# The first column of a block in the token mix, made by ScalarE instead of VectorE

## The chip, the core and the metric

The kernel runs on one core of one Trainium2 chip. The time is device microseconds from one launch to its end. The core's engines each work through their own queue of instructions in order: TensorE (PE in the profile, with its weight loads as PEld), VectorE (DVE), ScalarE (ACT), GpSimd (POOL), and SyncE (SP), which issues all the transfers here. An instruction that needs another engine's result waits at the head of its queue, and what stands behind it waits too.

## What is computed

One hybrid decoder layer on a sequence of 2048 tokens of width 1024, after an embedding layer norm: an input projection, RWKV-7 time mixing on eight heads, forgetting attention on eight heads, a SiLU gate, an output projection and a final layer norm. What matters here is the token mix of the projection's RWKV part: each token is mixed with the one before.

```python
h = x * (1.0 + scale[:, None, :]) + shift[:, None, :]
proj = h @ w_in
rw = proj[..., :RW_END]
rw_prev = jnp.pad(rw, ((0, 0), (1, 0), (0, 0)))[:, :-1]
rw = rw + (rw_prev - rw) * rwkv_mix        # r, k, v, and the two low-rank inputs
...                                        # decay, keys, scan over tokens, group norm
S = S * w_t - (S kk_t) b_t^T + v_t k_t^T   # the recurrence per head
```

## The kernel before

The sequence is worked in two halves of 1024 tokens, each half in two blocks of 512. The projection runs as tiles of 128 features by 512 tokens: 24 matmuls of 128x512 add up into one PSUM bank (three for each of eight slices of the inner dimension, since the operands are split into a rounded part and a rest). The tiles are written with features on partitions and tokens along the free axis, so "the token before" is the column to the left.

When the 24 matmuls of a tile are done, an evacuation stream takes the bank. For the parts r, k, v and the low-rank inputs this is `shift_mix` (line 901): ACT writes the bank times (1 - mix) into an SBUF slot of the tile `arena`; DVE adds the bank's columns 0 to 510 times mix to columns 1 to 511; DVE adds the last column of the block before, kept in the tile `car`, times mix to column 0; DVE copies the bank's column 511 into `car` for the next block; the bank is freed. `par("mix", g)` is a column of the tile `params`, one factor per partition. There are 13 feature groups, 2 halves and 2 blocks, so 52 calls. A weight tile is loaded by `weights` (line 818): a DMA into `wst`, an ACT cast into `wsp`, and a POOL subtraction (128x1024) that makes the rest; the projection matmuls read `ht` and `wsp`.

The recurrence (tiles `rw_s`, `rw_l`, `state`) runs beside the projection: per head group and block elementwise work, a triangular solve (`rwkv_solve`, line 1271: a long chain of small DVE instructions that ends in two transposes, then matmuls of 32x16 and of 32x32), and state updates by 64x64 matmuls (`rwkv_batch`, line 1361). Each pair of heads and half has two such solves, here called the first and the second of a pair. Attention works on `fx_s`, `fx_p` and `fx_v`.

No order is written by hand: a planner inside the kernel (`Driver`, from line 138) runs all streams as coroutines against a model of the engines. It gives each instruction a cost (`cost`, line 167) by engine, size, whether an operand lies in PSUM, and how many operands are pointers, adds a latency from one engine to another, and always goes on with the stream that is ready first. The order in which streams emit instructions is the order in which each engine's queue holds them. So a change of one instruction's engine changes the model's times, and with them the order of all that follows.

The program's calls go through one helper, so all instructions bear the line 134 and are told apart by tile names. `ps` is PSUM.

Of the kernel before, what the change touches and what calls it, by code (L numbers as in the profile page):

```python
# [12 lines left out]
AF = mybir.ActivationFunctionType  # L13
OP = mybir.AluOpType
# [274 lines left out]
def hymba_kernel(ctx: ExitStack, tc, x, c, emb_ln_g, emb_ln_b, w_ada, b_ada, w_in, rwkv_mix, w0,  # L289
# [3 lines left out]
    pe, act, dve, pool, sp = (Engine(drv, n, e) for n, e in (("pe", nc.tensor), ("act", nc.scalar),  # L293
                              ("dve", nc.vector), ("pool", nc.gpsimd), ("sp", nc.sync)))
# [73 lines left out]
    car = const.tile([128, 16], F32, name="car")  # L368
# [37 lines left out]
    def par(name, i=0):  # L406
        return params[:, off[name] + i:off[name] + i + 1]
# [493 lines left out]
    def shift_mix(b, g, o):  # L901

        act.activation(o, b.ap, AF.Copy, scale=pc[:, g:g + 1])
        yield
        dve.scalar_tensor_tensor(o[:, 1:512], b.ap[:, 0:511], par("mix", g), o[:, 1:512],
                                 op0=OP.mult, op1=OP.add)
        dve.scalar_tensor_tensor(o[:, 0:1], car[:, g:g + 1], par("mix", g), o[:, 0:1],
                                 op0=OP.mult, op1=OP.add)
        dve.tensor_copy(car[:, g:g + 1], b.ap[:, 511:512])
        b.free()  # L910
        yield

    def ev_low(b, half, p, blk):
        lo = yield from slots.get(1)
        yield from shift_mix(b, 12, lo.ap)
        act.activation(lo.ap[0:64], lo.ap[0:64], AF.Tanh)
        yield
        low[half, blk] = lo
# [60 lines left out]
    def ev_r(k, g0):  # L979
        def ev(b, half, p, blk):  # L980
            s = yield from slots.get(1)
            if blk:
                pending[0] -= 1
            if k == "g":
                yield from silu(b, s)
            else:
                yield from shift_mix(b, g0 + p, s.ap)
            res[half, p, k, blk] = s
        return ev
# [1069 lines left out]
```

## Time and profile before

| | us |
|---|---|
| three runs | 1901.69, 1914.04, 1914.87; median 1914.04 |
| the profiled execution | 1905.47 |
| its span, first to last instruction | 1903.7 |
| PE matmuls busy / PE weight loads | 1816.7 / 1307.2 |
| DVE busy | 1287.7 |
| ACT busy | 802.5 |
| POOL busy | 778.2 |
| mean granted clock of TensorE | 0.968 |

Busy times of different engines overlap, so they don't add up. The granted clock is a share of full speed: 1 is 2.4 GHz, 0.5 is 1.2 GHz, and a value between is a mean over both. The profiled execution is one run of its own, beside the three.

### The profile page before, as it was taken

What the parts mean: (1) busy time and instruction counts of PE and PEld (TensorE: products, weight loads), DVE (VectorE), ACT (ScalarE), POOL (GpSimd) and SP (SyncE); (2) the same over time, 40 slices, a digit from 0 to 9 for tenths busy, and PEclk for the clock granted to TensorE, in tenths of its full rate; (3) what the DMA queues carried; (4) which work ended last, traced back from release to release, by engine and by line L of the source; (5) the groups of instructions that cost most, each with busy time, mean ns of one, the idle gap of its engine ahead of it and who ended that gap; (6) DMA issues with size and microseconds to landing.
All of it is one profiled execution on the core that took longest, in us unless ns stands there. A gap on an engine that the chain in (4) does not pass through costs nothing. (4 is left out here: it accounts for less than half of the span.)

```text
span 1903.7 us, 35535 instructions
## 1 busy us (share of the span) xinstructions
PE 1816.7 (95%) x13609; PEld 1307.2 (69%) x13609; DVE 1287.7 (68%) x3049; ACT 802.5 (42%) x1573; POOL 778.2 (41%) x773
## 2 busy tenths in 40 slices
PE   8988999989999999999998999999999999999997
PEld 6766777767678657577776777777655557457775
DVE  6887376856645555857667764754678722897998
ACT  3454445554541543554554653452444431441000
POOL 2222341514222573624142333423456651485553
PEclk9999999999889999999999999999999999799999
DMA  9241110201116537232020111214433217413333
GB/s 293 66 123 52 42 53 21 64 24 45 61 42 188 171 115 234 84 118 72 13 72 24 46 39 40 72 56 129 125 116 107 87 62 251 157 62 121 133 134 105
DMA packets 172129, 181.60 MB, mean 95 GB/s; under 512 B 12180, under 2 KB 116197, under 8 KB 171960
## 3 DMA queue, kind: packets, MB, share of 16 engines
q1 hardware_dynamic: 171960, 179.33, 30.3%
q8 instruction: 108, 1.77, 0.4%
q14 instruction: 61, 0.50, 0.1%
HBM read 132.10 MB, written 47.13 MB: 94 GB/s over the span
## 5 line engine op out<-in xcount | busy, mean ns | idle before, releaser
L134 PE MATMUL ps<-ht,wsp 128*128 128x512 f32 x3840 | 985.9, 403 | 9.4 <-POOL wsp L134 7.5
L134 PEld LDWEIGHTS ps<-ht,wsp 128*128 128x128 f32 x3840 | 703.8, 190 | 167.6 <-issue 12.1
L134 POOL TENSOR_TENSOR wsp<-wst,wsp 128x1024 fp32r<-128x1024 f32 x79 | 195.4, 2473 | 331.0 <-ACT wsp L134 303.3
L134 ACT ACTIVATE rw_s<-ps 64x256 f32<-64x256 f32 (+3 forms) x544 | 215.6, 408 | 212.6 <-PE ps L134 111.9
L134 PE MATMUL ps<-rw_s 32*32 32x32 f32 (+4 forms) x5376 | 238.7, 227 | 34.1 <-DVE rw_s L134 26.3
L134 PEld LDWEIGHTS ps<-rw_s 32*32 32x32 f32 (+3 forms) x5376 | 207.9, 140 | 86.6 <-DVE rw_s L134 32.9
L134 PE MATMUL ps<-fx_s 67*128 67x512 f32 (+5 forms) x960 | 259.4, 393 | 2.4 <-DVE small L134 1.9
L134 PEld LDWEIGHTS ps<-fx_s 67*128 67x128 f32 (+1 forms) x960 | 167.0, 195 | 118.7 <-issue 65.9
L134 ACT ACTIVATE fx_p<-ps 128x512 f32<-128x512 f32 (+3 forms) x336 | 161.1, 521 | 175.0 <-PE ps L134 152.2
L134 POOL TENSOR_TENSOR fx_p<-fx_p 128x512 f32<-128x512 f32 (+2 forms) x160 | 184.9, 1162 | 114.9 <-PE ps L134 111.2
L134 DVE TENSOR_TENSOR rw_s<-rw_s 128x24 f32<-128x24 f32 (+11 forms) x544 | 164.3, 306 | 23.3 <-ACT rw_s L134 9.5
L134 POOL TENSOR_TENSOR small<-small,nhalf 128x8 f32<-128x8 f32 (+1 forms) x48 | 71.7, 1494 | 256.5 <-DVE small L134 171.9
L134 ACT ACTIVATE arena<-ps 128x512 f32<-128x512 f32 (+3 forms) x130 | 75.1, 579 | 230.5 <-PE ps L134 205.1
L134 DVE TENSOR_REDUCE small<-ps 128x1 f32<-128x512 f32 (+1 forms) x208 | 134.1, 683 | 43.0 <-PE ps L134 42.2
L134 PE MATMUL ps<-fx_p,fx_v 128*64 128x512 f32 (+3 forms) x640 | 160.2, 557 | 0.7 <-POOL fx_p L134 0.5
L134 DVE TENSOR_TENSOR fx_p<-fx_p 128x512 f32<-128x512 f32 (+1 forms) x128 | 107.4, 839 | 72.3 <-POOL fx_p L134 70.6
L134 ACT ACTIVATE wsp<-wst 128x1024 fp32r<-128x1024 f32 x80 | 84.2, 1052 | 145.7 <-DMA wst<-yscr 112.4
L134 DVE TENSOR_TENSOR arena<-ps,arena 128x512 f32<-128x512 f32 (+4 forms) x108 | 72.8, 675 | 77.5 <-ACT arena L134 58.5
L134 POOL TENSOR_TENSOR rw_s<-rw_s,arena 128x512 f32<-128x512 f32 x64 | 82.2, 1286 | 89.2 <-ACT rw_s L134 48.4
L134 DVE TENSOR_SCALAR state<-ps,dl 64x64 f32<-64x64 f32 x256 | 72.3, 283 | 64.5 <-PE ps L134 50.5
L134 POOL TENSOR_SCALAR rw_s<-rw_s 64x128 f32<-64x128 f32 x128 | 38.0, 296 | 114.0 <-PE ps L134 103.5
L134 ACT ACTIVATE rw_s<-rw_s 32x256 f32<-32x256 f32 (+2 forms) x112 | 69.8, 651 | 27.2 <-DVE rw_s L134 26.5
(152 smaller groups left out, 1888.4 us busy)
## 6 DMA issues: line engine op xcount, KB each, us to landing
wst<-in_w_in_dram SPq DMA_DIRECT2D x66, 512.0 KB
fx_s<-kscr SPq DMA_DIRECT2D x144, 128.0 KB
fx_s<-qscr SPq DMA_DIRECT2D x96, 128.0 KB
ada_t<-in_w_ada_dram SPq DMA_DIRECT2D x16, 512.0 KB
rw_l<-lowscr SPq DMA_DIRECT2D x32, 256.0 KB
kscr<-arena SPq DMA_DIRECT2D x32, 256.0 KB
qscr<-arena SPq DMA_DIRECT2D x32, 256.0 KB
arena<-in_x_dram SPq DMA_DIRECT2D x16, 512.0 KB
```

The lines of the kernel that those rows point to most:

```text
L134: return fn(*args, **kw)
```

## The change

The third instruction of `shift_mix` goes from DVE to ACT: an activation with the identity function, whose input is the kept column, whose scale is the mix factor and whose bias is the column 0 that ACT itself wrote before. The result goes to the same column.

```diff
     def shift_mix(b, g, o):
         act.activation(o, b.ap, AF.Copy, scale=pc[:, g:g + 1])
         yield
         dve.scalar_tensor_tensor(o[:, 1:512], b.ap[:, 0:511], par("mix", g), o[:, 1:512],
                                  op0=OP.mult, op1=OP.add)
-        dve.scalar_tensor_tensor(o[:, 0:1], car[:, g:g + 1], par("mix", g), o[:, 0:1],
-                                 op0=OP.mult, op1=OP.add)
+        act.activation(o[:, 0:1], car[:, g:g + 1], AF.Identity, scale=par("mix", g), bias=o[:, 0:1])
         dve.tensor_copy(car[:, g:g + 1], b.ap[:, 511:512])
         b.free()
         yield
```

On DVE, at the end of the second solve of the second pair in the first half (names: `rw_s` is the recurrence's tile, `ps` PSUM, in brackets the engines whose semaphores a row waits for), the queue held before:

```order
L134 TENSOR_TENSOR rw_s<-rw_s 128x2x4x2 [waits DVE_49]
L134 TENSOR_TENSOR rw_s<-rw_s 128x8 [waits DVE_49]
L134 TENSOR_TENSOR rw_s<-rw_s 128x2x4 [waits DVE_49]
L134 STREAM_TRANSPOSE rw_s<-rw_s 128x8x8x4 [waits DVE_49]
L134 SCALAR_TENSOR_TENSOR arena<-ps,params,arena 128x511 [waits Activation_49]
L134 SCALAR_TENSOR_TENSOR arena<-car,params,arena 128x1
L134 COPY car<-ps 128x1 [waits DVE_49]
L134 STREAM_TRANSPOSE rw_s<-rw_s 128x256
L134 TENSOR_TENSOR rw_s<-ps,rw_s 64x2x64 [waits PE_49]
```

And in the changed kernel, at the same solve:

```order
L134 TENSOR_TENSOR rw_s<-rw_s 128x2x4x2 [waits DVE_49]
L134 TENSOR_TENSOR rw_s<-rw_s 128x8 [waits DVE_49]
L134 TENSOR_TENSOR rw_s<-rw_s 128x2x4 [waits DVE_49]
L134 STREAM_TRANSPOSE rw_s<-rw_s 128x8x8x4 [waits DVE_49]
L134 TENSOR_TENSOR rw_s<-ps,rw_s 64x2x64 [waits PE_49]
L134 TENSOR_TENSOR rw_s<-ps,i_120 64x2x64
L134 TENSOR_TENSOR rw_s<-ps,rw_s 64x2x64
L134 TENSOR_TENSOR rw_s<-ps,i_120 64x2x64
L134 STREAM_TRANSPOSE rw_s<-rw_s 128x256 [waits DVE_49]
```

The token mix has left the place between the two transposes; four instructions that read PSUM stand there instead.

On ACT, at a place in the first half where token mixes meet the state updates (`arena<-ps,pc` is the token mix's first activation, `wsp<-wst` a weight cast), the queue held before:

```order
L134 ACTIVATE arena<-ps,pc 128x512
L134 ACTIVATE rw_s<-ps 64x256 x6
L134 ACTIVATE rw_s<-rw_s,params 128x512
L134 ACTIVATE rw_s<-ps 64x256 x2
L134 ACTIVATE arena<-ps,pc 128x512
L134 ACTIVATE wsp<-wst 128x1024
L134 ACTIVATE rw_s<-ps 128x512 x2
```

And in the changed kernel:

```order
L134 ACTIVATE arena<-ps,pc 128x512
L134 ACTIVATE rw_s<-ps 64x256 x4
L134 ACTIVATE arena<-car,arena,params 128x1
L134 ACTIVATE rw_s<-ps 128x128
L134 ACTIVATE rw_s<-ps 64x256 x8
```

The new activation stands in ACT's queue behind what the planner let in after the token mix's first activation: here four evacuations of the recurrence. The copy into `car` on DVE now waits for ACT (`COPY car<-ps 128x1 [waits Activation_49]` in all 52 places), where it waited for DVE alone before.

On PE, at the matmuls of that same second solve (`ht,wsp` are the projection, `rw_s` 32x16 and 32x32 the solve, `state` the state updates), the queue held before:

```order
L134 MATMUL ps<-ht,wsp 128x512 x6
L134 MATMUL ps<-rw_s 128x128 x4
L134 MATMUL ps<-rw_s 32x16 x32
L134 MATMUL ps<-state,rw_s 64x64 x2
L134 MATMUL ps<-rw_s,state 64x64 x2
L134 MATMUL ps<-ht,wsp 128x512 x3
L134 MATMUL ps<-rw_s 32x32 x48
L134 MATMUL ps<-state,rw_s 64x64 x2
```

And in the changed kernel:

```order
L134 MATMUL ps<-ht,wsp 128x512 x9
L134 MATMUL ps<-rw_s 32x16 x32
L134 MATMUL ps<-state,rw_s 64x64 x2
L134 MATMUL ps<-rw_s,state 64x64 x2
L134 MATMUL ps<-rw_s 128x128 x4
L134 MATMUL ps<-rw_s 32x32 x48
L134 MATMUL ps<-state,rw_s 64x64 x2
```

The group of three projection matmuls between the 32x16 and the 32x32 matmuls has moved ahead of the 32x16 ones. Over the whole queue this group is missing at six of the eight second solves now, and was missing at two before.

## Rows read from the trace of the kernel before

**Rows 1.** The page's first part: busy us, share, instructions of each engine.
```profile
span 1903.7 us, 35535 instructions
PE 1816.7 (95%) x13609; PEld 1307.2 (69%) x13609; DVE 1287.7 (68%) x3049; ACT 802.5 (42%) x1573; POOL 778.2 (41%) x773
```

**Rows 2.** Stretches: PE, PEld, DVE, ACT, POOL busy us, clock, DMA share, GB/s.
```profile
140.00:560.00 420.00, 395.11 (x4238) 302.70 (x4238) 269.49 (x803) 202.53 (x419) 137.13 (x149) 0.94 0.16 46
...
890.00:1280.00 390.00, 369.94 (x4162) 284.48 (x4160) 257.49 (x760) 197.08 (x408) 128.76 (x141) 0.97 0.16 46
...
1330.00:1560.00 230.00, 229.51 (x1043) 125.84 (x1042) 159.77 (x303) 103.00 (x211) 130.71 (x142) 1.00 0.32 98
```

**Rows 3.** Groups by form on DVE: busy us, mean ns, idle ahead.
```profile
L134 DVE SCALAR_TENSOR_TENSOR arena<-ps,params,arena 128x511 f32<-128x511 f32 x52 | 38.8, 746 | 37.7 <-ACT arena L134 37.3
...
L134 DVE SCALAR_TENSOR_TENSOR arena<-car,params,arena 128x1 f32<-128x1 f32 x52 | 29.0, 557 | 0.0
...
L134 DVE COPY car<-ps 128x1 f32<-128x1 f32 x52 | 8.2, 158 | 1.8
```

**Rows 4.** Instructions on the tile car: ns min/median/max, first and last start.
```profile
L134 DVE SCALAR_TENSOR_TENSOR arena<-car,params,arena x52: 197/209/2453, 66.8 to 1200.2; 128x1 f32<-128x1 f32 x52
```

**Rows 5.** Timeline 303 to 310 us: start us, us, engine, instruction, [idle before].
```profile
304.49 0.69 ACT L134 ACTIVATE arena<-ps,pc 128x512 f32<-128x512 f32 x1 [0.66 <-PE ps L134]
305.07 1.05 ACT L134 ACTIVATE wsp<-wst 128x1024 fp32r<-128x1024 f32 x1
...
305.86 0.75 DVE L134 SCALAR_TENSOR_TENSOR arena<-ps,params,arena 128x511 f32<-128x511 f32 x1
...
306.25 2.36 POOL L134 TENSOR_TENSOR wsp<-wst,wsp 128x1024 fp32r<-128x1024 f32 x1 [8.75 <-ACT wsp L134]
306.53 2.11 DVE L134 SCALAR_TENSOR_TENSOR arena<-car,params,arena 128x1 f32<-128x1 f32 x1
...
308.67 0.16 DVE L134 COPY car<-ps 128x1 f32<-128x1 f32 x1
...
308.74 0.43 DVE L134 STREAM_TRANSPOSE rw_s<-rw_s 128x256 f32<-128x256 f32 x1
...
309.23 0.73 PE L134 MATMUL ps<-rw_s 32*32 32x16 f32 x64 [1.17 <-DVE rw_s L134]
```

**Rows 6.** Waits, whole span: who for whom, us in total, times, longest.
```profile
PE ps L134 <- DVE rw_s L134: 26.3, 15, 3.6
...
ACT rw_s L134 <- PE ps L134: 121.9, 85, 5.3
```

**Rows 7.** Groups by form on ACT.
```profile
L134 ACT ACTIVATE rw_s<-rw_s 128x512 f32<-128x512 f32 x32 | 18.2, 618 | 0.0
...
L134 ACT ACTIVATE rw_s<-rw_s,pc,params 128x512 f32<-128x512 f32 x16 | 13.0, 811 | 6.4 <-DVE rw_s L134 6.0 <-issue 0.4
...
L134 ACT ACTIVATE dl<-rw_s 128x8 f32<-128x8 f32 x16 | 3.2, 202 | 0.0
```

**Rows 8.** Windows of 30 us around solver clusters, PE alone: busy us, granted clock.
```profile
150.80:180.80 30.00, 27.02 (x412) 0.94 0.13 37
...
381.20:411.20 30.00, 25.16 (x390) 0.89 0.07 19
412.50:442.50 30.00, 28.11 (x426) 1.00 0.08 20
...
528.80:558.80 30.00, 27.53 (x375) 0.72 0.13 37
...
1042.20:1072.20 30.00, 29.22 (x418) 1.00 0.12 36
1143.90:1173.90 30.00, 30.00 (x399) 1.00 0.13 41
```

**Rows 9.** Timeline of DVE at the first and the last long one.
```profile
276.02 1.35 DVE L134 SCALAR_TENSOR_TENSOR arena<-car,params,arena 128x1 f32<-128x1 f32 x1
...
277.49 0.68 DVE L134 TENSOR_TENSOR rw_s<-rw_s 128x512 f32<-128x512 f32 x1
...
1186.20 2.44 DVE L134 SCALAR_TENSOR_TENSOR arena<-car,params,arena 128x1 f32<-128x1 f32 x1
```

## The prediction

> **What bounds the kernel now.** I read the page's busy times first, then the busy time by stage, then the waits, then single stretches. TensorE (PE) is the bound: its matmuls cover 1816.7 of 1903.7 us, VectorE (DVE) is busy for 1287.7, ScalarE (ACT) for 802.5 [rows 1]. By stage the two recurrence stretches are the leaky ones: from 140 to 560 us PE is busy 395.11 of 420 at a granted clock of 0.94, from 890 to 1280 us 369.94 of 390 at 0.97, while in the attention stretch from 1330 to 1560 us it is busy 229.51 of 230 at 1.00 [rows 2]. A granted clock of 1 is the 2.4 GHz level; 0.94 means that some of the time was spent at 1.2 GHz, where half the work is done. So 25 + 20 us of PE idle, and some 25 + 12 us (0.06 x 420, 0.03 x 390) of clock, are all that can move there. The change touches only the token mix, whose last instruction starts at 1200.2 us [rows 4], so the recurrence stretches are where it must show. The largest wait of a PE matmul is for DVE on the recurrence's tiles: 26.3 us in 15 waits [rows 6]. A saving on DVE counts in those waits alone; elsewhere PE hides it.
>
> **What is removed from DVE.** 52 instructions of 128x1, together 29.0 us, mean 557 ns [rows 3]. The median is 209 ns and the longest 2453 [rows 4]: 52 x 0.209 = 10.9 us is work and 18.1 us is something else. The stretch at 306 us shows it: POOL starts the 2.36 us subtraction of a weight tile at 306.25; the 128x511 instruction before (0.75 us, first input in PSUM) runs through it, the 128x1 instruction, both of whose tensor inputs lie in SBUF, starts at 306.53 and takes 2.11 us, ending at 308.64, just behind POOL's end at 308.61; the copy behind it takes 0.16 as always [rows 5]. Eleven of the 52 are long like this, the first at 276.02 us, the last at 1186.20 [rows 9].
>
> The Trainium skill (SBUF — State Buffer, section Who interferes with whom) says that a VectorE instruction with two SBUF inputs contends with a GpSimd instruction that reads SBUF, and that the one that comes second waits for the whole of the first. The 306 us rows agree to 0.03 us. By that rule the hold would be passed on wherever the next DVE instruction has two SBUF inputs too, as it has at 277.49 [rows 9]; then less than the 18.1 us is gained on DVE.
>
> **What of it is on the path.** Three of the eleven (306.53, 413.83 and 926.52 us; the first stands for all) sit between the two transposes that end the triangular solve, and PE then waits 1.17 us for that DVE result [rows 5]. In the new order no token mix stands between these transposes, so the three waits should go: 3 x 1.17 = 3.5 us. The least is 0 (another DVE instruction is held instead), the most is the whole 26.3 us of rows 6, which is far, since the other twelve waits have none of these instructions right ahead of them. I take -3.5.
>
> **What is added to ACT.** 52 activations of 128x1 with scale and bias read from SBUF. No such instruction ran. The smallest on SBUF data, 128x8 without pointers, takes 202 ns; at 128x512 two pointers lift 618 to 811 [rows 7], 193 ns more. 202 + 193 = 395 ns, 52 of them 20.5 us. The lower bound is 202 ns (10.5 us), the upper 811 (42 us). ACT goes from 802.5 to some 823 us of 1904, 43%: 0 on the path, covered by the 95% of PE. If that cover were gone it would cost 20.5 us.
>
> The Trainium skill (ScalarE: Activation LUTs, section What ACT_TABLE_LOAD costs) gives 186 ns plus 0.833 per element plus about 93 per pointer operand, an estimate of 373 ns here, or 19.4 us. It speaks against the change: the new instruction is dearer than the 209 ns one it replaces.
>
> **The wait that is added.** The copy into `car` now waits for ACT, which must have read the old column. Behind it on DVE stand the bank's release and all later DVE work. On ACT the new activation comes directly behind the token mix's first activation in 15 of the 52 cases, behind a weight cast alone in 20, behind something else in 17. At 304.49 us the first activation, and at 305.07 a 1.05 us cast, would have let the new one end at 306.12 + 0.40 = 306.52, before the 128x511 instruction ends at 306.61 [rows 5]: no stall there. Where DVE is free at once, it ends its 0.75 us some 0.7 us before the new activation is done: at most 20 x 0.7 = 14 us of DVE standing, less than the 29.0 removed. Path: 0. The 17 others are the second rival.
>
> **What the planner moves.** The kernel's planner prices each instruction and orders all engines by it; the new prices redraw the order from the first token mix on. The matmul count is unchanged, so only idle and clock can change. I price the solver clusters (eight pairs, one pair per head group and half) by 30 us windows, as idle plus 30 x (1 - clock), all at full-speed value, which is an upper bound for the clock part [rows 8]:
> - first of a pair with few projection matmuls between (381.20): 4.84 + 3.3 = 8.1 us; with more between (150.80): 2.98 + 1.8 = 4.8 us. Five heavy and three light before; four heavy, two light and two in between now. Taking one heavy as light: -3.3 us.
> - second of a pair, with a projection group between the 32x16 and the forty-eight 32x32 matmuls (412.50): 1.89 + 0 = 1.9 us. Without it: 2.47 + 8.4 = 10.9 us (528.80) in one case, 0.78 + 0 = 0.8 us (1042.20) in the other. Before: four with, two without, two loose ones such as 1143.90 with 0. Now: none with, six without, two loose.
>
> Of the six bare ones four follow a group of nine projection matmuls, as the cheap one did, two a group of three or six, as the dear one did. So 4 x 0.8 + 2 x 10.9 = 25.0 now against 4 x 1.9 + 10.9 + 0.8 = 19.3 before: +5.7 us. Bounds: all cheap 4.8, -14.5; all dear 65.4, +46.1.
>
> **The sum.** -3.5 (solve) + 0 (ACT) + 0 (hand-off) - 3.3 + 5.7 = -1.1 us. The profiled execution took 1905.47 us, 1.77 beyond its span, so 1904.4. It lies 8.6 us under the median of the three runs, 1914.04, which reach from 1901.69 to 1914.87. A new median should fall between; I add half, 4.3, and forecast **1909 us**, no change: about 1%, 19 us, is what a measurement of this kernel can tell from none.
>
> **The rivals.**
> *The clock falls in the bare clusters (slower).* For it: 528.80, where the clock stood at 0.72; the new order makes six such places from two. Against: 1042.20, the same pattern at 1.00. Each dear cluster beyond my two adds 10.1 us. With three more, 1909 + 30.3 = 1939; with all six, 1909 + 40.4 = 1949. It decides from the third more on, since 1933 is 1% over.
> *DVE stands behind ACT (slower).* 17 new activations stand behind instructions that are not casts, some behind four 64x256 evacuations that wait for PE. ACT waits 121.9 us for PE on such tiles in 85 waits, longest 5.3 [rows 6], a mean of 1.43 us. 17 x 1.43 = 24 us of DVE standing, all on the path only if PE has nothing else: 1909 + 24 = 1933. At 5.3 us each it would be 90 us of standing. Against: projection matmuls stand behind most of these places, and DVE has 32% idle. It decides only if nearly all of it reaches PE.
> *The bare clusters are all cheap and the hold was dearer than seen (faster).* -14.5 for +5.7 is 20.2 less; with 9 us of the other DVE waits of rows 6 it gives 1909 - 29 = 1880; without them 1889. For it: 18.1 us of holds on DVE go, and only 3.5 are counted. Against: PE was not waiting at the other eight.
>
> **How the numbers follow.** No change 0.62 (its own range 1895 to 1930), clock slower 0.14, hand-off slower 0.08, faster 0.16. The 80% range leaves out half the dear and the 1880 case: 1888 to 1937. Faster by over 1% 0.17, same 0.61, slower 0.22.
>
> **What would show it.** Right: DVE's 29.0 us row is gone; an ACT row of 52 at about 395 ns; DVE busy near 1259 us; PE busy within 15 us of 1816.7; the waits of PE for DVE on the recurrence's tiles near 23 us; the granted clock at 0.96 to 0.975; attention unchanged. Wrong: a clock under 0.955 with six dips after the bare clusters (first rival); a large wait of DVE's `car` tile for ACT together with more PE waits for DVE (second); PE idle in the recurrence stretches under 30 us together (third).

## The result and the profile after

| | before | after |
|---|---|---|
| median of the runs made side by side, us | 1907.87 (1899.63 to 1914.87, 4 runs) | 1880.47 (1873.64 to 1885.43, 4 runs) |
| ratio after / before | | 0.9851, 95% interval 0.9806 to 0.9897 |
| profiled execution / its span, us | 1905.47 / 1903.7 | 1880.39 / 1878.7 |
| PE busy / PE idle in the span, us | 1816.7 / 87.0 | 1797.4 / 81.3 |
| mean granted clock | 0.968 | 0.977 |
| time at 1.2 GHz, 2 x (1 - clock) x span, us | 122 | 86 |

The change makes the kernel 1.5% faster. The forecast was 1909 us with a range from 1888 to 1937, so the result lies below the range, at the figure that the third rival had given (1880).

The last row of the table is used throughout. The granted clock has two levels, so a mean of 0.968 over 1903.7 us means 2 x 0.032 x 1903.7 = 122 us at 1.2 GHz; the third digit of the clock leaves about 2 us of doubt. One execution is a small sample of it: in 78 runs of the kernel before, made beside the experiments, it goes from 87 us (clock 0.977) to 166 (0.957), with a mean of 117. The four runs of after have a mean of 83. So below the mean over a kernel's runs stands beside the figure of its profiled execution.

The page's first part for the kernel after (answers to [rows 1]):

```profile
span 1878.7 us, 35539 instructions
PE 1797.4 (96%) x13609; PEld 1295.3 (69%) x13609; DVE 1270.7 (68%) x2997; ACT 819.6 (44%) x1625; POOL 776.7 (41%) x773
```

Here the main reading is that the span is shorter by 25.0 us, and that only 5.7 of these are PE idle time (87.0 to 81.3). The other 19.3 us are PE busy time, with the same 13609 matmuls. The same matmuls in less busy time means faster matmuls: the 36 us less at 1.2 GHz account for an estimated 15 to 18 of the 19.3 (0.43 us each by the last section, 0.5 if each counts half).

Stretches of after: busy us of PE, PEld, DVE, ACT and POOL, granted clock, DMA share, GB/s (answers to [rows 2]):

```profile
140.00:560.00 420.00, 398.25 (x4353) 306.12 (x4352) 268.88 (x802) 214.06 (x449) 142.01 (x153) 0.98 0.16 49
890.00:1280.00 390.00, 371.68 (x3996) 285.11 (x3995) 247.97 (x745) 202.71 (x426) 132.47 (x142) 0.97 0.15 46
1330.00:1560.00 230.00, 229.97 (x1085) 129.25 (x1084) 145.99 (x274) 104.64 (x212) 138.00 (x148) 1.00 0.31 94
```

The first recurrence stretch went from clock 0.94 to 0.98 and its idle from 24.9 to 21.75 us; the second stayed at 0.97 with 18.3 us of idle for 20.1. The attention stretch is as it was.

Groups by form of after (busy us, mean ns, idle ahead and who ended it), then the instructions on the tile `car` (ns min/median/max, first and last start), which answer to [rows 3, 4]:

```profile
L134 ACT ACTIVATE arena<-car,arena,params 128x1 f32<-128x1 f32 x52 | 19.7, 380 | 0.6
...
L134 DVE COPY car<-ps 128x1 f32<-128x1 f32 x52 | 7.9, 151 | 16.7 <-ACT arena L134 16.4
```

```profile
L134 ACT ACTIVATE arena<-car,arena,params x52: 368/380/390, 65.6 to 1181.2; 128x1 f32<-128x1 f32 x52
```

The new ACT instruction takes 380 ns and hardly varies (368 to 390), where the one on DVE ran from 197 to 2453. Its price is a new stall: DVE stands 16.4 us ahead of the copies into `car`, until ACT has read the old column.

Waits of after over the whole span: who for whom, us in total, times, longest (answers to [rows 6]):

```profile
PE ps L134 <- DVE rw_s L134: 28.5, 23, 2.6
...
DVE car L134 <- ACT arena L134: 16.4, 20, 2.2
```

PE's waits for DVE on the recurrence's tiles did not fall, they rose from 26.3 to 28.5 us. So the gain did not come by the way that the diff suggests, a shorter DVE queue in front of a waiting PE.

Where along the span the gain was made, the state updates of PE show, before and then after (ns min/median/max, first and last start):

```profile
L134 PE MATMUL ps<-state,rw_s x512: 217/241/369, 172.6 to 1293.3; 128*64 128x64 f32 x171
```

```profile
L134 PE MATMUL ps<-state,rw_s x512: 222/232/305, 172.1 to 1275.7; 128*64 128x64 f32 x171
```

The last one starts 17.6 us earlier, so about 7 of the 25.0 us come behind the recurrence, where the prediction had expected nothing to move.

Windows of 30 us from 4 us ahead of a solver cluster, PE alone, in the kernel after: busy us, granted clock (answers to [rows 8]):

```profile
265.50:295.50 30.00, 27.20 (x389) 0.83 0.10 28
...
409.60:439.60 30.00, 29.18 (x434) 1.00 0.10 29
520.70:550.70 30.00, 27.78 (x417) 0.94 0.11 31
...
905.90:935.90 30.00, 29.53 (x426) 1.00 0.07 20
```

The last three are bare second clusters. Priced as in the prediction (idle plus 30 x (1 - clock)), 409.60 costs 0.8, 905.90 costs 0.5, and 520.70 the most of all six, 2.2 + 1.8 = 4.0 us. The six together come to 7.85 us, where the prediction had 25.0.

### The profile page after: what moved, and what is told of

Its sections match the earlier page's. It is cut to its first block, busy times and chain, and to the rows that moved or that the text cites. A ratio compares the mean times of both kernels' runs of the same rounds, so it can differ in the third digit from the quotient of the medians.

```text
span 1878.7 us, 35539 instructions
## 1 busy us (share of the span) xinstructions
PE 1797.4 (96%) x13609; PEld 1295.3 (69%) x13609; DVE 1270.7 (68%) x2997; ACT 819.6 (44%) x1625; POOL 776.7 (41%) x773
## 4 chain that ended last, share of the span: by engine, by line
PE 66%; DVE 20%; ACT 5%; issue 4%; POOL 2%; DMA 2%; SPq 0%; POOLq 0%; DVEq 0%; ACTq 0%
PE ps L134 66%; DVE rw_s L134 9%; DVE arena L134 4%; ACT rw_s L134 3%; DVE small L134 3%; DVE end_s L134 3%; POOL wsp L134 1%; ACT arena L134 1%; ACT wsp L134 1%; DVE fx_p L134 1%; POOL rw_s L134 1%; DVE ht L134 1%; DMA end_s<-in_x_dram 1%; SPq L134 0%; DMA wst<-in_w_in_dram 0%
## 5 line engine op out<-in xcount | busy, mean ns | idle before, releaser
L134 DVE TENSOR_TENSOR rw_s<-rw_s 128x24 f32<-128x24 f32 (+11 forms) x544 | 176.6, 329 | 22.6 <-ACT rw_s L134 8.9
L134 PE MATMUL ps<-fx_p,fx_v 128*64 128x512 f32 (+3 forms) x640 | 156.4, 552 | 1.5 <-POOL fx_p L134 1.5
L134 DVE TENSOR_TENSOR arena<-ps,arena 128x512 fp32r<-128x512 f32 (+4 forms) x108 | 72.8, 675 | 64.0 <-ACT arena L134 61.2
```

The lines of the kernel that those rows point to most:

```text
L134: return fn(*args, **kw)
```

## The experiments

The diff changes two things at once: the engine that makes the column, and the price that the planner sees, with which it redraws the order of all engines. The theories told apart below: the **instruction** theory (DVE is no longer held by POOL, or the ACT hand-off costs less than that hold), the **order** theory (the redrawn order is better, by chance or by a cause), and, for the order, whether one drawing is luck or orders planned with ACT are better in general. In every edit `drv.time(...)` is the call that only tells the planner of an instruction, and `eng` is the engine behind the planner, which only emits it.

**1. The instruction without the order, the order without the instruction, neither.** In e1 the planner books the old DVE instruction, so the queues of PE, POOL and SP are those of before, and ACT makes the column. In e2 the planner books the ACT instruction and DVE makes the column.

```diff
# e1_act_old_order
-        dve.scalar_tensor_tensor(o[:, 0:1], car[:, g:g + 1], par("mix", g), o[:, 0:1],
-                                 op0=OP.mult, op1=OP.add)
+        drv.time(dve, "scalar_tensor_tensor", [o[:, 0:1], car[:, g:g + 1], par("mix", g), o[:, 0:1]], {})
+        act.eng.activation(o[:, 0:1], car[:, g:g + 1], AF.Identity, scale=par("mix", g), bias=o[:, 0:1])
# e2_dve_new_order
-        dve.scalar_tensor_tensor(o[:, 0:1], car[:, g:g + 1], par("mix", g), o[:, 0:1],
-                                 op0=OP.mult, op1=OP.add)
+        drv.time(act, "activation", [o[:, 0:1], car[:, g:g + 1], par("mix", g), o[:, 0:1]],
+                 dict(scale=par("mix", g), bias=o[:, 0:1]))
+        dve.eng.scalar_tensor_tensor(o[:, 0:1], car[:, g:g + 1], par("mix", g), o[:, 0:1],
+                                     op0=OP.mult, op1=OP.add)
# e3_none_old_order: as e1, with the drv.time line alone
```

> The first column is made on ACT, but the planner still plans with the price of the old DVE instruction, so every queue keeps the order of before (PE, POOL and SP row for row). Theory A (the redrawn order brought the gain): about 1904 us, within 5 us of before's 1908; PE's waits for DVE on the recurrence's tiles fall from 26.3 us by about 3.5, half-speed clock time stays near 123 us. Theory B (the instruction leaving DVE brought the gain, by itself): about 1880 us as in the changed kernel, half-speed time near 87 us.

> The first column stays on DVE, but the planner plans with the price and the waits of the ACT instruction, so every queue has the order of the changed kernel. Theory A (order): about 1882 us, half-speed time near 90 us. Theory B (instruction): about 1907 us, as before.

> The order of before, and the first column's instruction left out altogether (column 0 of each block isn't mixed): all that the 29.0 us of DVE can give in that order, with no ACT cost and no hand-off. Theory A: 1903 us, 4 to 5 below before. Theory B: 1880 us or less.

| | median us | ratio to before, 95% | span | PE busy | at 1.2 GHz, profiled | at 1.2 GHz, mean |
|---|---|---|---|---|---|---|
| e1, ACT, old order | 1898.70 | 0.9942 (0.9910 to 0.9974) | 1891.5 | 1805.6 | 91 | 105 (10 runs) |
| e2, DVE, new order | 1879.06 | 0.9839 (0.9759 to 0.9918) | 1877.7 | 1789.6 | 64 | 68 (4 runs) |
| e3, left out, old order | 1890.77 | 0.9892 (0.9828 to 0.9957) | 1889.3 | 1808.2 | 102 | 95 (4 runs) |

The page's first part of e2, its row of the old instruction (group by form), and DVE, POOL and the copy around one hold (timeline: start us, us, engine, instruction):

```profile
span 1877.7 us, 35536 instructions
PE 1789.6 (95%) x13609; PEld 1289.6 (69%) x13609; DVE 1284.0 (68%) x3049; ACT 803.3 (43%) x1573; POOL 777.2 (41%) x773
```

```profile
L909 DVE SCALAR_TENSOR_TENSOR arena<-car,params,arena 128x1 f32<-128x1 f32 x52 | 24.5, 472 | 0.0
```

```profile
932.15 1.29 POOL L134 TENSOR_TENSOR rw_s<-rw_s,arena 128x512 f32<-128x512 f32 x1
...
932.83 2.97 DVE L909 SCALAR_TENSOR_TENSOR arena<-car,params,arena 128x1 f32<-128x1 f32 x1
933.40 2.38 POOL L134 TENSOR_TENSOR wsp<-wst,wsp 128x1024 fp32r<-128x1024 f32 x1
...
935.84 0.16 DVE L134 COPY car<-ps 128x1 f32<-128x1 f32 x1
```

e2 still has the instruction on DVE, still held by POOL: the one that starts at 932.83 us lasts through two POOL instructions in a row and ends 0.02 us behind the second. 24.5 us are busy for 10.9 us of work (52 x 0.209), so 13.6 us of holds are left, where before had 18.1. The kernel is as fast as after all the same (mean of after less mean of e2: 0.3 us, 95% interval -8 to 8; intervals of differences are worked out here and below from the spread of the two kernels' runs). With the new order given, moving the instruction is worth nothing that can be told; the order alone gives the whole gain.

In the old order the instruction does count. The waits of PE for DVE and of the copy for ACT in e1, and the stretch that [rows 5] shows for the kernel before:

```profile
PE ps L134 <- DVE rw_s L134: 22.4, 12, 3.6
...
DVE car L134 <- ACT arena L908: 12.4, 20, 1.6
```

```profile
306.96 0.75 DVE L134 SCALAR_TENSOR_TENSOR arena<-ps,params,arena 128x511 f32<-128x511 f32 x1
...
307.33 2.37 POOL L134 TENSOR_TENSOR wsp<-wst,wsp 128x1024 fp32r<-128x1024 f32 x1 [8.39 <-ACT wsp L134]
...
307.89 0.39 ACT L908 ACTIVATE arena<-car,arena,params 128x1 f32<-128x1 f32 x1
...
308.31 0.16 DVE L134 COPY car<-ps 128x1 f32<-128x1 f32 x1 [0.60 <-ACT arena L908]
308.39 0.43 DVE L134 STREAM_TRANSPOSE rw_s<-rw_s 128x256 f32<-128x256 f32 x1
```

ACT's instruction runs through POOL's subtraction without being held. DVE's second transpose starts 1.43 us after the 128x511 instruction began, where it was 2.88 us in before (305.86 to 308.74). The waits of PE for DVE fall from 26.3 in 15 to 22.4 in 12: three waits and 3.9 us, which is the prediction's -3.5. But the median fell by 0.58%, 11 us, and the profiled span by 12.2 us. The rest is in part clock: time at 1.2 GHz fell from 122 to 91 us in the two profiled executions, but only from 117 to 105 in the means (95% interval of the fall 1 to 23). At 0.4 us of time for each us at 1.2 GHz, the run-to-run figure of the last section, these 12 us are an estimated 5 of the 11; with the 3.9 us of waits some 2 us are left unexplained.

e3 takes the column out altogether and is 20 us faster than the runs of before beside it (median 1910.68). So in the old order the DVE instruction cost some 20 us, of which the prediction counted 3.5. The intervals of the ratios of e1 and e3 overlap, but their runs hardly do: 1887.47 to 1891.20 us for e3, 1890.38 to 1910.54 for e1, a difference of the means of 9.1 us (95% interval 4.7 to 13.4). In the old order the column on ACT therefore still costs about 9 us more than no column. Whether that is ACT's own time or the 12.4 us that the copy waits was not tested. Nor do the two halves of the change add up: order alone 30 us, instruction alone 11, both together 27.

**2. The hand-off.** The 16.4 us that DVE stands ahead of the copy can be taken away without touching the order: the last column goes into two tiles in turn, so that the copy never has to wait for ACT's reading.

```diff
# e4_two_car_new_order (the planner books what it books in after)
+    car2 = const.tile([128, 16], F32, name="car2")
+    cars, turn = (car, car2), [0] * 16
...
+        was, nxt = cars[turn[g] % 2], cars[(turn[g] + 1) % 2]
+        turn[g] += 1
+        act.eng.activation(o[:, 0:1], was[:, g:g + 1], AF.Identity, scale=par("mix", g), bias=o[:, 0:1])
...
+        dve.eng.tensor_copy(nxt[:, g:g + 1], b.ap[:, 511:512])
```

> The changed kernel in its own order, with the last columns kept in two tiles in turn, so that DVE's copy never waits for ACT. In the changed kernel DVE stands 16.4 us in 20 waits at that copy. If this hand-off costs anything on the path: 1 to 8 us less than the changed kernel's 1880. If PE covers it: 1880, within 2 us.

The copies' row in e4 (group by form), where the idle time ahead of them is gone:

```profile
L915 DVE COPY car<-ps 128x1 f32<-128x1 f32 x52 | 7.6, 146 | 0.0
```

1881.63 us, ratio 0.9847 (0.9781 to 0.9914), after being 0.9851. The standing went from 16.7 us to 0.0 and the time did not move: the means differ by 1.4 us, with a 95% interval from 7 us less to 10 us more for e4. So in the new order the hand-off has no cost that can be told, as predicted; a few us are not excluded. In the old order it was not tried.

**3. Is the order luck?** Changing one latency of the planner by a few ns draws a new order, as the change's price did. Each of four such numbers was run twice, with the column on DVE as in before and on ACT as in after; here the planner books what is emitted.

```diff
-LATENCY = dict(pe=197.0, act=165.0, dve=130.0, pool=100.0, sp=0.0)
+LATENCY = dict(pe=197.0, act=165.0, dve=137.0, pool=100.0, sp=0.0)   # m2
+LATENCY = dict(pe=197.0, act=165.0, dve=124.0, pool=100.0, sp=0.0)   # m5
+LATENCY = dict(pe=197.0, act=158.0, dve=130.0, pool=100.0, sp=0.0)   # m6
+LATENCY = dict(pe=197.0, act=165.0, dve=131.0, pool=100.0, sp=0.0)   # l2
```

> A fifth order with the column on DVE: the planner's latency behind a DVE instruction is 131 instead of 130. Theory A: 1875 to 1925. Theory C: 1895 to 1925.

> A fifth order with the column on ACT, the same figure moved (131). Theory A: 1875 to 1925. Theory C: 1875 to 1895.

> The kernel before, with one figure of the planner's model moved: the latency it adds behind a DVE instruction is 137 instead of 130. No instruction changes, only the order on all engines is redrawn. If the time of an order is a matter of the draw (theory A): anywhere from 1875 to 1930 us. If orders planned with the column on DVE are slower as a kind (theory C): 1900 us or more.

> The changed kernel with the same figure moved (137 instead of 130): another order with the column on ACT. Theory A: anywhere from 1875 to 1930 us, without regard to the instruction. Theory C: 1890 us or less.

> The kernel before, with the planner's latency behind DVE at 124 instead of 130: a third draw with the column on DVE. Theory A: 1875 to 1930 us. Theory C: 1900 us or more.

> The changed kernel with the planner's latency behind DVE at 124: a third draw with the column on ACT. Theory A: 1875 to 1930 us. Theory C: 1890 us or less.

> A fourth order with the column on DVE: the planner's latency behind an ACT instruction is 158 instead of 165. So far orders with the column on DVE gave 1909, 1920 and 1891 us. Theory A (each order is a draw, the kind says nothing): 1875 to 1925. Theory C (orders planned with the column on DVE are slower as a kind): 1895 to 1925.

> A fourth order with the column on ACT, the same figure moved (158). So far 1880, 1879 and 1902 us. Theory A: 1875 to 1925. Theory C: 1875 to 1895.

| drawing | on DVE: median, ratio (95%), at 1.2 GHz (profiled / mean) | on ACT: the same |
|---|---|---|
| the two kernels | 1909.3 (78 runs beside the experiments), 1, 122 / 117 | 1880.47, 0.9851 (0.9806 to 0.9897), 86 / 83 |
| l2 | 1895.24, 0.9921 (0.9892 to 0.9949), 106 / 107 | 1881.28, 0.9855 (0.9825 to 0.9885), 83 / 81 |
| m2 | 1920.09, 1.0059 (1.0031 to 1.0087), 123 / 125 | 1879.31, 0.9862 (0.9811 to 0.9913), 60 / 73 |
| m5 | 1890.67, 0.9895 (0.9841 to 0.9950), 117 / 95 | 1901.75, 0.9971 (0.9937 to 1.0004), 103 / 113 |
| m6 | 1927.51, 1.0083 (1.0043 to 1.0123), 143 / 130 | 1892.85, 0.9925 (0.9899 to 0.9952), 91 / 99 |

The runs of before lay beside each group of experiments, with medians from 1906.5 to 1910.68, so two rows compared by their medians have some 4 us of doubt. The drawing alone moves the time by up to 37 us on DVE (1890.67 to 1927.51) and 22 us on ACT. One pair, m5, goes the other way. Over the five, DVE has a mean of 1908.6 with a standard deviation of 15.7, ACT 1887.1 with 9.8: a difference of 21.4 us with a standard error of sqrt((15.7² + 9.8²) / 5) = 8.3. With five drawings each that is a 95% interval of 2 to 41 us, and of -4 to 47 when the drawings are taken in pairs. So the 27 us of the change are not sure to come back in another drawing: that some 20 us belong to planning with ACT is likely and not shown, and 10 to 16 us either way belong to the drawing. No drawing beats the kernel after by more than the spread of its own runs (1873.64 to 1885.43).

**4. The instruction in other orders.** The edits of e1 and e2 on top of m2 and m6: the order planned for DVE with ACT making the column (s1, s2), and the order planned for ACT with DVE making it (s3, s4).

> The order of m6_dve (1927.5 us, the slowest of ten) with the column's instruction on ACT, all other queues unchanged. If the order makes the time: 1920 to 1930. If the instruction does, in orders planned for DVE: 12 to 20 us less, 1907 to 1916, as in the order of before.

> The order of m2_dve (1920 us), which has no token mix between the two transposes that end a solve, with the column's instruction on ACT. If the order makes the time: 1915 to 1922. If the instruction does: 1900 to 1908. If its place between the transposes is what made it cost 12 us in the order of before: 1915 to 1922, since here there is none.

> The order of m6_act (1893 us) with the column's instruction back on DVE, all other queues unchanged. If the order makes the time: 1888 to 1898. If the instruction does: 1905 or more.

> The order of m2_act (1879 us) with the column's instruction back on DVE. If the order makes the time: 1876 to 1884. If the instruction does: 1891 or more.

| order | column on DVE | column on ACT | ACT less DVE (95% interval for the means) |
|---|---|---|---|
| of before | 1909.3 | 1898.70 (e1) | -11 (-14 to -6) |
| of m2_dve | 1920.09 | 1909.40 (s2, 0.9992, 0.9956 to 1.0027) | -11 (-17 to -7) |
| of m6_dve | 1927.51 | 1907.37 (s1, 0.9982, 0.9944 to 1.0019) | -20 (-27 to -10) |
| of after | 1879.06 (e2) | 1880.47 | +1 (-8 to +8) |
| of m2_act | 1881.95 (s4, 0.9866, 0.9805 to 0.9926) | 1879.31 | -3 (-9 to +10) |
| of m6_act | 1894.49 (s3, 0.9939, 0.9906 to 0.9972) | 1892.85 | -2 (-6 to +5) |

In all three orders planned for DVE the instruction's move is worth 11 to 20 us, in the three planned for ACT nothing that can be told. PE's waits for DVE do not explain it. Mean clock, engine totals, and PE's waits for DVE, of m6_dve and then of s1:

```profile
core 0: 1927.5 us, clock 0.963
...
PE 1824.8 (95%) x13609; PEld 1312.6 (68%) x13609; DVE 1284.5 (67%) x3049; ACT 801.1 (42%) x1573; POOL 786.6 (41%) x773
...
PE ps L134 <- DVE rw_s L134: 28.0, 14, 4.1
```

```profile
core 0: 1899.3 us, clock 0.976
...
PE 1804.5 (95%) x13609; PEld 1299.0 (68%) x13609; DVE 1262.7 (66%) x2997; ACT 816.0 (43%) x1625; POOL 784.4 (41%) x773
...
PE ps L134 <- DVE rw_s L134: 26.3, 12, 4.1
```

The waits for DVE fell by 1.7 us and the span by 28.2: 20.3 of it is PE busy time, which is mostly clock, and 7.9 is PE idle (102.7 to 94.8), most of it in other waits. The two executions overstate the clock: time at 1.2 GHz fell from 143 to 91 us in them and from 130 to 103 in the means, an estimated 11 us of the 20. In the order of m2 the means fell from 125 to 112 (the interval includes 0), an estimated 5 us of the 11. So clock is a part of it, and what else is not shown. Nor is it the place that the prediction named: m2_dve has no token mix between the two transposes of any solve, and still gains 11 us. The size of the hold doesn't tell either. The old instruction's rows in m2_dve, where its move is worth 11 us, and in s4, where it is worth nothing that can be told (the order of m2_act):

```profile
L134 DVE SCALAR_TENSOR_TENSOR arena<-car,params,arena 128x1 f32<-128x1 f32 x52 | 31.1, 599 | 0.0
```

```profile
L909 DVE SCALAR_TENSOR_TENSOR arena<-car,params,arena 128x1 f32<-128x1 f32 x52 | 26.0, 500 | 0.0
```

By 52 x 0.209 = 10.9 us of work that is 20.2 us of holds in the one and 15.1 in the other; the cost differs more than the hold.

**5. The planner's price as the cause.** The planner books the DVE instruction without POOL's hold: its `cost` gives 192 ns, where the mean in [rows 3] is 557. For the ACT one it gives 281, where 380 was measured. If planning with too low a price is what makes the DVE orders bad, a planner that books 557 ns for it should draw good ones. The edit prices eight more DVE instructions of one column so, those of the tile `pc` within the first 60 us.

```diff
     # cost(), p1_dve_priced; p2_m6dve_priced has act=158.0 too
+            if op == "scalar_tensor_tensor" and n == 1:
+                return 557.0
```

> The column on DVE as before, the planner's price for this instruction raised to the 557 ns of the trace; the order is redrawn. If the too low price makes the orders planned for DVE slow: 1895 us or less. If the price isn't the cause: 1891 to 1928, as the five orders planned with the column on DVE so far.

> The same with the planner's latency behind ACT at 158 as in m6_dve (1928 us). If the price is the cause: 1895 us or less. If not: 1891 to 1928.

Measured were 1890.56 us (0.9914, 0.9894 to 0.9933) and 1890.27 (0.9906, 0.9875 to 0.9937), 68 and 79 us at 1.2 GHz (70 and 80 in the means). Both lie 16 to 19 us under before (1906.92 beside them, 1909.3 over all), as the price as cause would have it, with the column on DVE throughout. But of the five orders without that price m5 lies as low (1890.67) and l2 nearly (1895.24), so with two drawings it is supported and not shown.

## Why the prediction was wrong, point by point

**Removed from DVE: right, but DVE's total was not.** The 29.0 us row is gone. DVE was to be busy near 1259 us and was for 1270.7, 17.0 us less than before and not 29: the hold was partly passed on. In e1, with the order of before, DVE is busy 21.4 us less (1287.7 to 1266.3 in its page). Which instructions took it over in after was not worked out.

**Added to ACT: right.** 52 instructions of 380 ns, 19.7 us, against 395 ns and 20.5 us forecast. The Trainium skill (ScalarE: Activation LUTs, section What ACT_TABLE_LOAD costs), from which the prediction worked out an estimate of 373 ns, was nearer still. In the new order ACT at 819.6 us is not on the path: with some 16 us more to do than in e2 (803.3) it made nothing slower. In the old order e1 is 9 us slower than e3, so there the zero is not confirmed.

**The added wait: right in the new order.** DVE stands 16.4 us in 20 places. These are not the twenty cases behind a cast that were bounded by 14 us: those have about 6.7 us, and nine of the seventeen others have about 10, where the second rival had up to 24. e4 shows no cost of it, and the second rival falls with it for this order.

**The direct wait on the solve: right in size, too small in what it was taken for.** The term was -3.5 us for three waits of PE; in the order of before the change took away 3 waits and 3.9 us. But the kernel of that order gained 11 us in the median, and 20 with the column left out. The step that failed is "a saving on DVE counts in those waits alone". With the waits went time at 1.2 GHz, 12 us in the means (117 to 105), an estimated 5 us of the time, of which the sum had nothing.

**What the planner moves: the step that failed most.** The sum had -3.3 + 5.7 for the solver clusters. Measured by the same windows, the first clusters cost 46.7 us in after and 48.3 in before (-1.6), the second ones 8.0 and 24.4 (-16.4): -18.0 in all, out of the 25.0 that the span lost. The mis-sized term is that of the six bare clusters, 25.0 forecast and 7.85 measured. Two of them were booked at 10.9 us each, on the strength of one window of the kernel before (528.80, clock 0.72), taken for a property of the pattern. The base was mis-sized too: the second clusters of before cost 24.4 and not the 19.3 of the sum, since the four with a projection group were not all as cheap as the one row (412.50) that stood for them. The dear cluster can be seen again, behind the same PE queue, in the profiled executions of e1 and of e3 (windows of 30 us, PE busy, granted clock):

```profile
519.00:549.00 30.00, 27.28 (x415) 1.00 0.12 37
```

```profile
519.00:549.00 30.00, 27.42 (x369) 0.72 0.12 37
```

The first is e1, the second e3. Behind the same queue of PE the clock stood at 1.00 once and at 0.72 once. PE had been idle for about the same 2.6 to 2.7 us in both. What a dip costs was well taken from the row; whether it comes can't be read from one execution. That DVE differs in e1 and e3 (one waits for ACT, one has no column to wait for) stays a reservation; that the total varies by itself, from 87 to 166 us at 1.2 GHz, the 78 runs of the one kernel show. The -18.0 us are read from one execution of each kernel, so on which clusters they fall is in part chance. In total the two executions are typical: 36 us less at 1.2 GHz, 34 in the means.

**A redrawn order as a sum of small differences.** The prediction gave a redrawn order a mean of +2.4 us (the -3.3 and +5.7) and bounds from -14.5 to +46.1, and its range ended 21 us below the forecast. e2 shows -30 us by the order alone, and the five drawings with DVE spread over 37 us. An order drawn anew is a term with a spread of some 10 to 16 us, and that spread belonged into the range on both sides.

**The third rival: right time, half its reason.** Bare clusters nearly all cheap is what happened (7.85 us, where it had 4.8), and the time is the 1880 us that it gave. But its other half (9 us of PE's waits for DVE) did not: those waits are 28.5 us, and the sign that was named for it, PE idle under 30 us in the recurrence stretches together, did not show (21.75 + 18.3 = 40). The profiled gain came mostly as clock, PE busy 19.3 us down where the prediction allowed 15, for which no rival had a row to watch other than the first, on the losing side. That the time agreed to the us is luck.

**The base: right.** Half the offset from the profiled execution to the median, +4.3, gave 1909 for no change; 78 runs of before made beside the experiments have a median of 1909.3.

**What stays open.** Why the redrawn order has less time at 1.2 GHz: e2 shows that the order brings the gain, not what in the order does. Whether orders planned for DVE have more of it as a kind (115 us against 90 in the mean over the five drawings each). And why in the three tried, and in none of the three planned for ACT, the held instruction costs 11 to 20 us. Counted in the program orders, token mixes between the two transposes of a solve are 4, 4, 0, 1 and 3 in the DVE orders (before, l2, m2, m5, m6) and 0 in all five ACT orders, but m2 with none is among the slowest. An underpriced instruction, behind which the planned order arrives late at many small places, would fit p1 and p2; it is argued, not shown.

## What to carry to other kernels

Where a planner orders the program by its prices, an edit that changes a price is two changes: time the new order with the old instruction, and the new instruction in the old order, before either gets the credit, and give the order a spread from several drawings rather than a sum of its pieces. Compare PE busy time at an equal matmul count: where it falls, the gain is clock, and waits alone will undercount it. One dip of the clock in one profile is a price, not a place: look for it in a second execution before it is multiplied, and compare kernels by the mean clock of all their runs.

## What the runs showed of the hardware

- The run-to-run spread of this kernel is mostly clock. Over 78 runs of before, from 1897.83 us (granted clock 0.976) to 1928.02 (0.957), time and clock go together with a correlation of -0.94, at 15.6 us for each 0.01 of clock, which is 0.40 us for each us at 1.2 GHz.
- Over the kernels here, PE busy rises by about 0.40 us for each us at 1.2 GHz: m2_act has 60 us of it and 1791.9 us busy, m6_dve 143 and 1824.8, so (1824.8 - 1791.9) / (143 - 60) = 0.40. A line through all twenty profiled executions gives 0.43.
- A DVE instruction of 128x1 that works for 0.2 us took up to 2.97 us in e2 and 3.71 in m6_dve, each time through two POOL instructions in a row, and holds of 13.6 us in all cost nothing that can be measured in one order (e2) and with 18.5 us (m6_dve, 29.4 busy) some 20 us in another. A hold has no price apart from the order in which it stands.
- The ACT instruction of the same size, with all operands in SBUF too, took 0.39 us in the middle of a POOL instruction of 2.37 us, and never more than 390 ns in the 52 of after.
